# Spectra kept in DRAM twice, once for each half of the partitions, in the hyena stage of a Fourier and Hyena layer

## The chip, the cores and the metric

The kernel runs on one core of a Trainium2 chip. The metric is the device time of one execution in microseconds. Three runs of the kernel before gave 2331.82, 2333.49 and 2336.78; the median, 2333.49, is the time before.

## The reference

One layer works on x of 2048 positions and 1024 channels, in float32. After an RMS norm and an input projection, 512 channels go through a two-dimensional Fourier transform and 512 through a Hyena mixer: two rounds of a gated long convolution, each with a filter that is as long as the sequence. Both results are normed and projected out, added to x, and a feed-forward part with a squared ReLU and a last norm follow. What the change touches is the long convolution:

```
def implicit_filters(l, w0, b0, w_inner, b_inner, freq, w_out):
    z, t = positional_features(l)
    ...
    h = jnp.sin(fr * (z @ w0.astype(f32) + b0.astype(f32)))
```

The filters come out of a small network of the position and a decay over time, in two directions, are normed by their sum of squares, and are convolved with the gated input by way of their spectra: transform of the input, product with the filter's spectrum, inverse transform. The kernel computes the spectra once per group of 128 channels and per round, and reads them again when the input is convolved.

## The kernel before

**Two stages.** The function `filters` makes the filters and their spectra in eight units (four groups of 128 channels, `ct`, times two rounds, `n`). The function `hyena` makes the convolutions in eight blocks of the same groups and rounds. Between the two the spectra lie in DRAM, in the scratch tensors `kd` ("spec" in the profile).

**A unit of the filters.** `generate(q)`, q from 0 to 7, makes an eighth of the unit's filter: a load of the decay (`dec`, one for two q, L170 under the helper `load`), four matmuls (`pk`, L504, on TensorE, PE), a product with the decay on VectorE (DVE; `kt`, L508), a split in a high and a low part (a cast to `kh` on ScalarE, ACT, L181; the rest `kl`, L182, on DVE for even q and on GpSimd, POOL, for odd q), a square on ACT (`sqr`, L518; it has one buffer) and its sum on POOL (`acc`, L519). Behind the last q two folds on POOL end the sum (L521, L522). `normalise` then takes that sum through a matmul (`psum_k`, L528) and some small operations on DVE (`vk`, L530, and further). `skip` puts the result into the filter's first element (`pdk`, L544). `stage1(c)`, c from 0 to 7, makes three matmuls each (L189 to L191) and a transpose on DVE (`Gk`, L418). `stage2(q)` makes four matmuls (`pk2`, L572; "pk" in the profile, which leaves digits out), a copy to `ks` on ACT (L575), and for every second q a store to DRAM (L577).

**The order of the filters.** While unit i runs its eight steps of stage one and eight of stage two, the products of unit i + 2 are generated at steps given by a table, `GENERATE`. For units 1 to 5 the norm of unit i + 1 is made at step q = 1 of stage two; for unit 6 at c = 4 of stage one. From unit 5 on the gates are loaded to `zz` (L623) and scaled on POOL and DVE in turns (L557). All loads and stores go out on SyncE (SP), in order. Each engine runs its instructions in the order in which the compiled program has them; that order is drawn up for each kernel by a scheduler, so that it can move where only a transfer is edited.

**A block of the hyena stage.** `first(c)` transforms the input (L666), `second(q)` takes four frequencies at a time: `spectrum(q)` loads `ks` (L652; four buffers), four matmuls make `pz` (L673), ACT makes the turned copy `zs` (L676, L677), and y = pz * ks[0] + zs * ks[1] is made by DVE (L679), POOL (L680) and one of the two (L681). `inverse(q)` (L689) needs y and runs three steps behind `second`. `turn` and `gate` end the block during the next one. In block 7, the last, no first stage of another block lies beside this. Behind it the output projection begins (`pt_y`, L785, out of `yf`, which is loaded and normed on ACT, L802).

**The form of the spectra.** A spectrum as stage two leaves it lies in 128 partitions, 32 x 128 numbers in each; partitions 0 to 63 hold one part of it and partitions 64 to 127 the other (the product treats them as a real and an imaginary part). In the block `ks[:, 0]` holds the one part and `ks[:, 1]` the other, and both are needed in partitions 0 to 63 as well as in 64 to 127. So each half of the partitions is loaded with the same 256 KB, by two transfers.

Of the kernel before, what the change touches and what calls it, by code (L numbers as in the profile page):

```python
# [10 lines left out]
F32 = mybir.dt.float32  # L11
# [116 lines left out]
P = 128  # L128
# [6 lines left out]
def hybrid_block(ctx: ExitStack, tc: tile.TileContext, A, out):  # L135
    nc = tc.nc
# [4 lines left out]
    def scratch(name, shape):  # L141
        return dram.tile(shape, F32, tag=name, name=name)

    gd = [scratch(f"gates{i}", [P, NT, 512]) for i in range(3)]
    kd = [[scratch(f"spec{i}{n}", [P, 32, 128]) for n in range(2)] for i in range(4)]
    wfd = scratch("wfd", [1024, 512])
    embd = scratch("embd", [P, 32, P])
    xtd = [scratch(f"xt{t}", [P, 8, P]) for t in range(NT)]
# [13 lines left out]
    def pool(name, side="left"):  # L162
        return tc.tile_pool(name=name, bufs=1, side=side, reuse_waits="tile")

    def pa(nm):
        return ps.tile([P, 512], F32, tag="a", name=nm, bufs=8)
# [304 lines left out]
    def filters(ctx, fp, gp, zp, zzs, norms, emb, wo, e1k, f2):  # L471
# [9 lines left out]
        p = pa("plongd")  # L481
# [3 lines left out]
        class Unit:  # L485
# [83 lines left out]
            def stage2(self, q):  # L569
                p = pa("pk2")  # L570
                for j in range(4):
                    nc.tensor.matmul(p[:, 128 * j : 128 * j + 128], lhsT=f2[:, 4 * q + j, :], rhs=self.G[:, :, 4 * q + j], start=True, stop=True)  # L572
                if q % 2 == 0:
                    self.ks = sp.tile([P, 8, 128], F32, tag="ks", name="ks", bufs=3)
                nc.scalar.copy(self.ks[:, 4 * (q % 2) : 4 * (q % 2) + 4, :], p.rearrange("p (f c) -> p f c", f=4))  # L575
                if q % 2:
                    nc.sync.dma_start(kd[self.ct][self.n][:, 4 * q - 4 : 4 * q + 4, :], self.ks)  # L577

        units = [Unit(ct, n) for n in range(2) for ct in range(4)]
        for u in units[:2]:  # L580
# [7 lines left out]
        sp = ctx.enter_context(pool("spectra", "right"))  # L588
# [41 lines left out]
    def hyena(hp, wp, rp, zz, e1, b1, f2, a2, out_weights, out_ahead):  # L630
# [6 lines left out]
        class Block:  # L637
# [9 lines left out]
            def spectrum(self, q):  # L647

                ks = hp.tile([P, 2, 4, 128], F32, tag="ks", name="ks", bufs=4)
                src = kd[self.ct][self.n][:, 4 * q : 4 * q + 4, :].rearrange("(s p) f c -> p s f c", s=2)  # L650
                for hf in (slice(0, 64), slice(64, 128)):
                    nc.sync.dma_start(ks[hf], src)  # L652
                if q == 0:

                    nc.scalar.copy(ks[64:65, 0, 0, :], ks[64:65, 1, 0, :])
                    for h in (0, 64):
                        nc.gpsimd.memset(ks[h : h + 1, 1, 0, :], 0.0)
                return ks
# [742 lines left out]
```

## Time and profile before

| what | before |
|---|---|
| median of three runs | 2333.49 us |
| the profiled execution | 2339.88 us |
| its span | 2336.8 us |
| mean granted TensorE clock | 0.986 |
| stores of spectra | 32 of 512 KB, first issued at 484.7 us, last at 637.5 us |
| loads of spectra | 128 of 256 KB, first issued at 638.0 us, last at 840.2 us |
| HBM read, written | 312.54 MB, 152.27 MB |

The span is the stretch of the profile in which the core works; all times of views count from its start. A group in the profile is a line of the kernel, an engine, an operation and its tiles (out<-in), then how often, busy time and the mean of one in ns, and the idle time of the engine just before such instructions with what ended it. In the view of waits a row tells which engine waited at which line, for whom, how long in total, how often, and the longest. In the timeline a row has its start, its duration, and in brackets how long the engine had been idle and what released it.

### The profile page before, as it was taken

To read this page: it belongs to the slowest core of one execution; us is meant where nothing else is said; L and a number is where in the kernel's file an instruction comes from. 1 tells how busy PE (TensorE), PEld (TensorE's weight loads), DVE (VectorE), ACT (ScalarE), POOL (GpSimd) and SP (SyncE) were. 2 spreads that over 40 slices of the span, in tenths; PEclk is the share of its full clock that TensorE was granted. 3 is DMA by queue.
4 is the path that set the end of the run, shared out by engine and by line. 5 is a ranking of instruction groups with operands and counts; after the bars stand their busy time and mean duration, and the time that the engine had idled before them with its cause. 6 is when DMAs were issued, how large, how long until landed. Compare 5 with 4: busy or idle time off the path is not lost. (4 is left out here: it accounts for less than half of the span.)

```text
span 2336.8 us, 31028 instructions
## 1 busy us (share of the span) xinstructions
PE 2250.9 (96%) x11025; PEld 1860.4 (80%) x11025; DVE 1514.5 (65%) x2248; ACT 1106.6 (47%) x1826; POOL 840.6 (36%) x633
## 2 busy tenths in 40 slices
PE   7999998999899979998999999999999999999998
PEld 6887787799787858886788877888888888888886
DVE  6998666677577774547544457444466666866667
ACT  6554211466455554544555556555543333533334
POOL 3345322567465522215755556555400000000000
PEclk9999999999999989999999999999999999999999
DMA  7535888457688986567544456444479666866631
GB/s 250 181 137 176 290 308 321 144 199 233 214 201 188 200 218 189 177 182 237 161 150 152 152 204 208 152 150 149 149 279 373 234 191 198 284 207 193 198 117 72
DMA packets 294780, 468.42 MB, mean 200 GB/s; under 512 B 18453, under 2 KB 142687, under 8 KB 290273
## 3 DMA queue, kind: packets, MB, share of 16 engines
q1 hardware_dynamic: 291265, 460.43, 61.9%
q10 hardware_dynamic: 3360, 6.02, 0.8%
q8 instruction: 86, 1.41, 0.3%
q14 instruction: 69, 0.57, 0.1%
HBM read 312.54 MB, written 152.27 MB: 199 GB/s over the span
## 5 line engine op out<-in xcount | busy, mean ns | idle before, releaser
L181 ACT CAST qahm<-ra 128x1024 fp32r<-128x1024 f32 x110 | 116.0, 1054 | 345.8 <-PE p2u L190 172.0
L182 DVE TENSOR_TENSOR qalm<-ra,qahm 128x1024 fp32r<-128x1024 f32 x110 | 134.7, 1224 | 154.8 <-ACT qahm L181 151.7
L1183 POOL TENSOR_TENSOR acc<-acc,gfin 128x512 f32<-128x512 f32 x4 | 5.1, 1278 | 632.9 <-DMA out<-acc 625.4
L189 PE MATMUL pu<-wh,xh 128*128 128x512 f32 x512 | 206.4, 404 | 5.8 <-ACT wh L184 4.8
L190 PE MATMUL pu<-wl,xh 128*128 128x512 f32 x512 | 203.3, 397 | 5.9 <-DVE wl L182 3.7
L191 PE MATMUL pu<-wh,xl 128*128 128x512 f32 x512 | 203.2, 397 | 5.7 <-DVE xl L182 5.7
L190 PE MATMUL p2u<-qblm,qahm 128*128 128x512 f32 x504 | 196.2, 389 | 0.3 <-DVE qblm L182 0.3
L189 PE MATMUL p2u<-qbhm,qahm 128*128 128x512 f32 x504 | 195.9, 389 | 0.0
L191 PE MATMUL p2u<-qbhm,qalm 128*128 128x512 f32 x504 | 195.8, 389 | 0.0
L397 POOL TENSOR_TENSOR acc<-acc,cw 128x512 f32<-128x512 f32 x45 | 60.9, 1353 | 206.1 <-DVE acc L374 204.8
L182 DVE TENSOR_TENSOR qblm<-rb,qbhm 128x1024 fp32r<-128x1024 f32 x110 | 134.0, 1219 | 1.1 <-ACT qbhm L181 1.1
L181 ACT CAST ahm<-s 128x512 fp32r<-128x512 f32 x124 | 76.7, 621 | 94.0 <-PE p1v L190 54.1
L190 PEld LDWEIGHTS pu<-wl,xh 128*128 128x128 f32 x512 | 98.3, 192 | 28.7 <-DVE wl L182 4.1
L191 PEld LDWEIGHTS pu<-wh,xl 128*128 128x128 f32 x512 | 98.2, 192 | 28.3 <-DVE xl L182 7.7
L189 PEld LDWEIGHTS pu<-wh,xh 128*128 128x128 f32 x512 | 98.0, 192 | 27.8 <-ACT wh L184 6.2
L182 POOL TENSOR_TENSOR alm<-W,ahm 128x512 fp32r<-128x512 f32 x63 | 85.5, 1358 | 91.4 <-ACT ahm L181 91.4
L181 ACT CAST qbhm<-rb 128x1024 fp32r<-128x1024 f32 x110 | 115.3, 1048 | 4.6 <-DMA a1m<-c 2.8
L190 PEld LDWEIGHTS p2u<-qblm,qahm 128*128 128x128 f32 x504 | 94.6, 188 | 20.3 <-DVE qblm L182 0.8
L189 PEld LDWEIGHTS p2u<-qbhm,qahm 128*128 128x128 f32 x504 | 94.6, 188 | 20.2 <-issue 0.3
L191 PEld LDWEIGHTS p2u<-qbhm,qalm 128*128 128x128 f32 x504 | 94.6, 188 | 19.6
L181 ACT CAST ahm<-W 128x512 fp32r<-128x512 f32 x94 | 57.6, 615 | 103.4 <-PE p1u L190 100.8
L191 PE MATMUL p1u<-bm,alm 128*128 128x512 f32 x252 | 99.9, 396 | 6.4 <-DVE alm L182 6.4
(387 smaller groups left out, 6456.8 us busy)
## 6 DMA issues: line engine op xcount, KB each, us to landing
W<-in_w_fc SPq DMA_DIRECT2D x66, 512.0 KB, 4.6
ks<-spec SPq DMA_DIRECT2D x128, 256.0 KB, 6.8
rb<-td SPq DMA_DIRECT2D x64, 512.0 KB, 4.1
ra<-a1m SPq DMA_DIRECT2D x56, 512.0 KB, 6.0
ra<-a0m SPq DMA_DIRECT2D x54, 512.0 KB, 10.7
rb<-in_w_fc SPq DMA_DIRECT2D x46, 512.0 KB, 4.5
f<-in_w_fc SPq DMA_DIRECT2D x16, 1024.0 KB
td<-f SPq DMA_DIRECT2D x16, 1024.0 KB, 4.7
```

The source lines that it names most:

```text
L181: nc.scalar.copy(hi, src)
L182: (eng or nc.vector).tensor_sub(lo, src, hi)
L189: nc.tensor.matmul(o, lhsT=lh, rhs=rh, start=start, stop=False, skip_group_check=more)
L190: nc.tensor.matmul(o, lhsT=lh, rhs=rl, start=False, stop=False, skip_group_check=more)
L191: nc.tensor.matmul(o, lhsT=ll, rhs=rh, start=False, stop=stop, skip_group_check=more)
L397: nc.gpsimd.tensor_add(m1, m1, cw[:, 3, :])
L1183: nc.gpsimd.tensor_mul(acc[i][:, c], acc[i][:, c], gfin[:, c])
```

## The change

The scratch tensor of a spectrum gets another form, [2, 64, 8, 2, 512], and holds everything twice: the first index h is the half of the partitions that will read it, then come 64 partitions, eight q, the half s of the spectrum, and 512 numbers (four frequencies of 128 channels). In `stage2` each q has a `ks` tile of its own, half as wide as before and with six buffers in place of three. Its two halves of 64 partitions are stored by one transfer each, which reads its source twice (a broadcast over h) and writes 64 x 2 runs of 2 KB. In `spectrum` one transfer takes the place of two: for each of the 128 partitions one run of 4 KB that holds both halves of four frequencies.

So 32 stores of 512 KB become 128 stores of 256 KB, and 128 loads of 256 KB become 64 of 512 KB. SP issues 32 transfers more in all. Lines behind the new empty line have a number higher by one in the changed kernel up to the loads.

```diff
-    kd = [[scratch(f"spec{i}{n}", [P, 32, 128]) for n in range(2)] for i in range(4)]
+
+    kd = [[scratch(f"spec{i}{n}", [2, 64, 8, 2, 512]) for n in range(2)] for i in range(4)]
...
-                if q % 2 == 0:
-                    self.ks = sp.tile([P, 8, 128], F32, tag="ks", name="ks", bufs=3)
-                nc.scalar.copy(self.ks[:, 4 * (q % 2) : 4 * (q % 2) + 4, :], p.rearrange("p (f c) -> p f c", f=4))
-                if q % 2:
-                    nc.sync.dma_start(kd[self.ct][self.n][:, 4 * q - 4 : 4 * q + 4, :], self.ks)
+                ks = sp.tile([P, 1, 512], F32, tag="ks", name="ks", bufs=6)
+                nc.scalar.copy(ks[:, 0], p)
+                for s in range(2):
+                    part = ks[64 * s : 64 * s + 64].broadcast_to([64, 2, 512])
+                    nc.sync.dma_start(kd[self.ct][self.n].rearrange("h p q s x -> p h q s x")[:, :, q, s], part)
...
-                src = kd[self.ct][self.n][:, 4 * q : 4 * q + 4, :].rearrange("(s p) f c -> p s f c", s=2)
-                for hf in (slice(0, 64), slice(64, 128)):
-                    nc.sync.dma_start(ks[hf], src)
+                src = kd[self.ct][self.n].rearrange("h p q s x -> (h p) q (s x)")[:, q]
+                nc.sync.dma_start(ks.rearrange("p s f c -> p (s f c)"), src)
```

The order on PE is the same in both kernels. On DVE, ACT, POOL and SP it changes from unit 1 of the filters to the end of the hyena stage. Three places are shown.

First DVE, around the start of stage one of unit 4 in the kernel before. Gk_4981 is the tile of unit 4's transposes, kt_4946 and kt_4972 are the last two products (q = 6 and 7) of unit 5, and kt_5012 to kt_5070 the first four of unit 6.

```order
L508 TENSOR_TENSOR kt_4946<-pk_4941,dec_4939 128x512
L182 TENSOR_TENSOR kl_4771<-kt_4946,kh_4770 128x4x8x16
L508 TENSOR_TENSOR kt_4972<-pk_4967,dec_4939 128x512
L418 STREAM_TRANSPOSE Gk_4981<-pk1_4982 128x8x2x32
...
L508 TENSOR_TENSOR kt_5012<-pk_5007,dec_5005 128x512
L418 STREAM_TRANSPOSE Gk_4981<-pk1_5019 128x8x2x32
L182 TENSOR_TENSOR kl_5003<-kt_5012,kh_5002 128x4x8x16
...
L508 TENSOR_TENSOR kt_5034<-pk_5029,dec_5005 128x512
L508 TENSOR_TENSOR kt_5058<-pk_5053,dec_5051 128x512
L508 TENSOR_TENSOR kt_5070<-pk_5065,dec_5051 128x512
```

The same place in the changed kernel. Gk_5045 is unit 4's tile there; kt_4936 to kt_5036 are the products q = 4 to 7 of unit 5, and vk_5161 is made of psum_k, the norm of unit 5.

```order
L419 STREAM_TRANSPOSE Gk_5045<-pk1_5046 128x8x2x32
L419 STREAM_TRANSPOSE Gk_5045<-pk1_5051 128x8x2x32
L509 TENSOR_TENSOR kt_4936<-pk_4931,dec_4929 128x512
L509 TENSOR_TENSOR kt_4966<-pk_4961,dec_4929 128x512
L419 STREAM_TRANSPOSE Gk_5045<-pk1_5056 128x8x2x32
L183 TENSOR_TENSOR kl_4819<-kt_4936,kh_4818 128x4x8x16
...
L419 STREAM_TRANSPOSE Gk_5045<-pk1_5110 128x8x2x32
L509 TENSOR_TENSOR kt_5006<-pk_5001,dec_4999 128x512
L509 TENSOR_TENSOR kt_5036<-pk_5031,dec_4999 128x512
L183 TENSOR_TENSOR kl_4819<-kt_5006,kh_4818 128x4x8x16
L531 TENSOR_SCALAR vk_5161<-psum_k_5159 128x1
```

The products q = 4 and 5 of unit 5 moved from ahead of unit 4's first transpose to behind its second, and q = 6 and 7 to behind its last, directly ahead of the norm that needs their squares. Units 2, 3 and 5 have q = 6 and 7 at the same place.

Second ACT, at the same stretch of the program, before: casts and squares of the same products (kh_4770, sqr_4950 and sqr_4976), of the first ones of unit 6 (kh_5002), and the first two copies of unit 4's stage two (ks_5082, twice).

```order
L181 CAST kh_4770<-kt_4946 128x4x8x16
L518 ACTIVATE sqr_4950<-kt_4946 128x512
L575 COPY ks_4958<-pk2_4953 128x512
L575 COPY ks_4958<-pk2_4960 128x512
L181 CAST kh_4770<-kt_4972 128x4x8x16
L518 ACTIVATE sqr_4976<-kt_4972 128x512
...
L575 COPY ks_5082<-pk2_5077 128x512
L518 ACTIVATE sqr_5074<-kt_5070 128x512
L575 COPY ks_5082<-pk2_5084 128x512
```

In the changed kernel, where kh_4818 is unit 5's tile, and ks_5146 and ks_5155 are the first two copies of unit 4's stage two:

```order
L182 CAST kh_4818<-kt_4936 128x4x8x16
L519 ACTIVATE sqr_4940<-kt_4936 128x512
L182 CAST kh_4818<-kt_4966 128x4x8x16
L519 ACTIVATE sqr_4970<-kt_4966 128x512
L575 COPY ks_5146<-pk2_5141 128x512
L575 COPY ks_5155<-pk2_5150 128x512
L182 CAST kh_4818<-kt_5006 128x4x8x16
L519 ACTIVATE sqr_5010<-kt_5006 128x512
L182 CAST kh_4818<-kt_5036 128x4x8x16
L519 ACTIVATE sqr_5040<-kt_5036 128x512
```

The last two casts and squares of unit 5 moved from ahead of unit 4's stage one to behind its first two copies of stage two.

Third POOL, at the norm that unit 6 makes at c = 4 of its stage one, for unit 7. Before, acc_5256 is unit 7's sum of squares and zz_5402 the gates; the last sum and the two folds end it.

```order
L519 TENSOR_TENSOR acc_5256<-acc_5256,sqr_5378 128x512
L557 TENSOR_TENSOR zz_5402<-zz_5402,norms_3591 128x4x128 x2
L519 TENSOR_TENSOR acc_5256<-acc_5256,sqr_5399 128x512
L182 TENSOR_TENSOR kl_5255<-kt_5424,kh_5254 128x4x8x16
L519 TENSOR_TENSOR acc_5256<-acc_5256,sqr_5428 128x512
L521 TENSOR_TENSOR acc_5256<-acc_5256 128x256
L522 TENSOR_TENSOR acc_5256<-acc_5256 128x128
L557 TENSOR_TENSOR zz_5402<-zz_5402,norms_3591 128x4x128 x2
```

In the changed kernel the sum is acc_5336, sqr_5445 to sqr_5520 are the squares of its last four products, and zz_5492 the gates.

```order
L520 TENSOR_TENSOR acc_5336<-acc_5336,sqr_5445 128x512
L183 TENSOR_TENSOR kl_5335<-kt_5462,kh_5334 128x4x8x16
L520 TENSOR_TENSOR acc_5336<-acc_5336,sqr_5466 128x512
L520 TENSOR_TENSOR acc_5336<-acc_5336,sqr_5489 128x512
L183 TENSOR_TENSOR kl_5335<-kt_5516,kh_5334 128x4x8x16
L520 TENSOR_TENSOR acc_5336<-acc_5336,sqr_5520 128x512
L558 TENSOR_TENSOR zz_5492<-zz_5492,norms_3591 128x4x128
L522 TENSOR_TENSOR acc_5336<-acc_5336 128x256
L558 TENSOR_TENSOR zz_5492<-zz_5492,norms_3591 128x4x128
L523 TENSOR_TENSOR acc_5336<-acc_5336 128x128
L558 TENSOR_TENSOR zz_5492<-zz_5492,norms_3591 128x4x128 x6
```

The two scalings of zz that stood together ahead of the last two sums stand between the folds now. On DVE the products of which these squares are made stood ahead of unit 6's first transpose before, and stand behind its fifth now. On SP, the load of the inverse transform's matrix (a2) stood ahead of the stores of units 6 and 7 and stands behind all stores now, directly ahead of the loads of spectra; the reads of yf (L776, L778) moved from behind the last load to the second block.

## The prediction

> **What bounds the kernel now.** The page's first part comes first: TensorE (PE) is busy for nearly the whole span, so time can only be won or lost where PE waits.
>
> ```profile
> span 2336.8 us, 31028 instructions
> PE 2250.9 (96%) x11025; PEld 1860.4 (80%) x11025; DVE 1514.5 (65%) x2248; ACT 1106.6 (47%) x1826; POOL 840.6 (36%) x633
> ```
>
> The change touches two stages, which the windows view separates: the filters (stores, about 484 to 637 us) and the hyena blocks (loads, 638 to 860 us). Its columns: stretch, then busy time of PE, PEld, DVE, ACT, POOL, the granted clock, the share of the DMA engines, GB/s.
>
> ```profile
> 500.00:560.00 60.00, 60.00 (x459) 55.33 (x458) 42.83 (x81) 38.77 (x79) 44.91 (x38) 1.00 0.63 210
> 600.00:620.00 20.00, 12.99 (x69) 10.14 (x69) 11.77 (x23) 6.62 (x14) 10.04 (x9) 0.83 0.48 176
> 640.00:840.00 200.00, 188.22 (x1314) 163.55 (x1312) 150.41 (x234) 110.67 (x192) 116.55 (x104) 0.99 0.88 198
> 840.00:860.00 20.00, 13.68 (x64) 9.39 (x64) 10.58 (x21) 6.95 (x16) 5.08 (x4) 0.74 0.98 261
> ```
>
> In the filters PE has no gap at all from 500 to 560 us; every wait added there is added to the end. In the hyena blocks PE lacks 11.8 us up to 840 and 6.3 us in the last 20, with the DMA engines at 0.88 and 0.98. The waits view of 640 to 870 us says on what (engine and line waited, releaser: us in total, times, longest):
>
> ```profile
> PE pv L689 <- DVE y L681: 16.0, 15, 3.8
> PE pt_y L785 <- ACT yf L802: 4.1, 2, 3.1
> POOL zs L680 <- DMA ks<-spec: 30.6, 18, 6.0
> DVE y L679 <- DMA ks<-spec: 12.1, 13, 3.5
> PE pv L689 <- DVE y L681: 7.3, 7, 1.6
> ```
>
> The last line is the same view for 830 to 855 us alone. PE waits for y, and y's two inputs wait for the spectra, so the loads are what is late.
>
> **The loads (gain).** Today a load of four frequencies is two DMAs, each to 64 partitions. In the list of DMA issues (KB each, us to landing) they stand beside two transfers between DRAM and 128 partitions in runs of 4 KB, which is the new load's form:
>
> ```profile
> ks<-spec SPq DMA_DIRECT2D x128, 256.0 KB, 6.8
> spec<-ks SPq DMA_DIRECT2D x32, 512.0 KB, 3.7
> dec<-in_decay SPq DMA_DIRECT2D x32, 512.0 KB, 4.0
> ```
>
> The new load should land in about 4.0 us, as dec does, while it moves both halves. Per byte it should also hold the engines for less. In 500 to 560 us, where all traffic is of 128 partitions, a share of 0.63 moves 210 GB/s, 333 GB/s at full share. In 640 to 840 us, mostly 64-partition loads, 0.88 moves 198, 225 at full share. So 512 KB hold the engines for 2.3 us now and 1.6 us then. With that, y should come in time. The 8.7 us that PE waits for y before 830 go (16.0 less 7.3). Of the 7.3 us in the last block, which has no first stage to cover its chain of y, I take half, 3.6. The changed order issues the reads of yf and their norm in the second block instead of behind the last load, so the 4.1 us at pt_y go too. With 0.6 us for matmuls at a lower clock after such waits I take -17. Bounds: -4 (only pt_y), and -24 (16.0 + 4.1 and all 4 us or so of slow clock, which the 0.74 in the last slice suggests).
>
> **The stores: the order they make (loss).** The arithmetic of each step stays. The copy to ks is 128x512 as before, and the second copy of the spectra is made by the DMA. But 128 small stores in place of 32 lie ahead of the loads of dec on SP, and the order of DVE, ACT and POOL is drawn up anew round them. In units 2 to 5 the last products kt (q6 and q7) of the unit after now stand behind all eight transposes of this unit on DVE, and their casts and squares behind the first two ks copies on ACT (the rows of order in the section on the change). Before, they stood ahead of the transposes. Yet PE's order is as it was: after the second group of stage two comes psum_k, which needs the sum of all squares. PE's timeline of unit 1 gives the clock of a unit (start, us, ...):
>
> ```profile
> 491.94 0.48 PE L189 MATMUL pk<-k,e1h 128*128 128x512 f32 x1
> ...
> 499.41 1.95 PE L504 MATMUL pk<-wo,emb 128*128 128x128 f32 x16
> ...
> 502.98 0.28 PE L528 MATMUL psum_k<-ones,acc 128*128 128x1 f32 x2
> ```
>
> Count from a unit's first matmul: stage one is through at 7.5 us, and psum_k, behind two groups of stage two, is asked for at 11.0. Durations for the chain come from the groups of 484 to 640 us (busy, mean ns):
>
> ```profile
> L519 POOL TENSOR_TENSOR acc<-acc,sqr 128x512 f32<-128x512 f32 x40 | 52.3, 1307 | 12.5 <-ACT sqr L518 12.5
> L418 DVE STREAM_TRANSPOSE Gk<-pk 128x512 f32<-128x512 f32 x56 | 37.9, 702 | 4.7 <-PE pk L191 4.7
> L575 ACT COPY ks<-pk 128x512 f32<-128x512 f32 x63 | 35.0, 579 | 11.7 <-PE pk L572 11.6
> L508 DVE TENSOR_TENSOR kt<-pk,dec 128x512 f32<-128x512 f32 x44 | 29.6, 675 | 9.1 <-PE pk L504 6.8 <-ACT ks L575 1.2 <-POOL kl L182 0.8
> L518 ACT ACTIVATE sqr<-kt 128x512 f32<-128x512 f32 x40 | 25.3, 632 | 15.7 <-POOL acc L519 15.7
> L182 POOL TENSOR_TENSOR kl<-kt,kh 128x512 fp32r<-128x512 f32 x19 | 24.9, 1311 | 11.2 <-ACT kh L181 11.2
> L181 ACT CAST kh<-kt 128x512 fp32r<-128x512 f32 x36 | 22.3, 618 | 25.8 <-DVE kt L508 25.8
> L557 POOL TENSOR_TENSOR zz<-zz,norms 128x512 f32<-128x512 f32 x8 | 12.5, 1581 | 10.4 <-ACT norms L553 9.8 <-PE pk L572 0.6
> L521 POOL TENSOR_TENSOR acc<-acc 128x256 f32<-128x256 f32 x6 | 4.4, 737 | 0.5
> L522 POOL TENSOR_TENSOR acc<-acc 128x128 f32<-128x128 f32 x6 | 3.3, 548 | 0.5
> ```
>
> The eighth transpose ends at 8.4 us, kt of q6 and q7 at 9.1 and 9.8. That is early enough, but ACT must first copy ks of q0 and q1, the second of them at 11.0 to 11.6. Then cast to 12.2, square to 12.9; POOL adds to 14.2, splits q7 (1.31) to 15.5, adds its square to 16.8, and folds in 0.74 and 0.55 to 18.1. PE waits from 11.0 to 18.1. Successive operations overlap a little, so I take 7.0. Nothing of PE's is left to fill it: the next matmuls stand behind psum_k. DVE too has its next products behind the result (vk). So it comes again in each of units 2 to 5.
>
> The trace has one such wait already, in unit 6, with what follows it on PE:
>
> ```profile
> 599.27 0.48 PE L189 MATMUL pk<-kh,e1h 128*128 128x512 f32 x1
> ...
> 602.39 0.40 PE L190 MATMUL pk<-kl,e1h 128*128 128x512 f32 x1
> 609.21 0.59 PE L528 MATMUL psum_k<-ones,acc 128*128 128x1 f32 x2 [6.20 <-POOL acc L522]
> ...
> 610.65 0.63 PE L191 MATMUL pk<-kh,e1l 128*128 128x512 f32 x1
> ...
> 613.21 0.58 PE L191 MATMUL pk<-kh,e1l 128*128 128x512 f32 x1
> ```
>
> The 14 matmuls of stage one before it follow each other by 0.24 us (3.12 us for 13 steps, between the first two rows), those behind it by 0.43 (2.56 us for 6 steps, between the last two; the slice's clock is 0.83). For the nine matmuls of the three groups that end at 613 that is 9 x 0.19 = 1.7 us, lost behind a wait of this length. Units 2 to 5: 4 x (7.0 + 1.7) = **+35**. Bounds 20 (5 us each, no slow clock) and 40.
>
> In unit 6 psum_k is asked for 3.7 us after the unit's start and ran at 9.9 (609.21 less 599.27). Before, all eight kt stood ahead of this unit's transposes on DVE; now five transposes stand ahead of the last four kt. The fifth ends at 4.4, kt of q4 at 5.1, cast and square at 6.3. From there POOL is the chain, as its order shows: four sums and two splits (6 x 1.31; the third sum starts 0.7 late, behind a square that waits for its one buffer) to 14.8, then zz, fold, zz, fold (1.58 + 0.74 + 1.58 + 0.55) to 19.2. **+9**; bounds 5 and 12.
>
> **The stores as transfers.** They double from 16.8 to 33.6 MB, read 64 partitions at a time. The DMA view of 484 to 640 us and of 640 to 840 us, and SP's issues:
>
> ```profile
> q1 hardware_dynamic: 16095, 33.78, 64.0%
> q1 hardware_dynamic: 32014, 39.34, 87.2%
> L577 SPq DMA_DIRECT2D spec<-ks x32: 319/320/1562, 484.7 to 637.5; - x32
> L652 SPq DMA_DIRECT2D ks<-spec x128: 573/605/4610, 638.0 to 840.2; - x128
> ```
>
> At 333 GB/s the stage's 33.8 + 16.8 MB need 152 us of engine time. If reads from 64 partitions go like today's writes to 64 (225 GB/s), it is 33.6/225 + 17.0/333 = 200 us. The stage lasts 153 us now and with the waits above some 197, so either nearly fits. SP issues 128 x 0.6 = 77 us in that time. What stays is the end: unit 7 makes its 16 stores (4.2 MB) in about 7 us, and a2 (2.1 MB) comes behind all of them, where it stood ahead of them before. That is 6.3 MB, 19 to 25 us at the two rates, ahead of the first load of spectra: 12 to 18 us more than the 7 us in which they are made, 8 to 14 more than the 4 us that it takes to land. The first y was multiplied at 647.3 while the load was issued at 638.0:
>
> ```profile
> 647.28 0.65 DVE L679 TENSOR_TENSOR y<-pz,ks 128x512 f32<-128x512 f32 x1
> ```
>
> With a landing of 4 to 5 us some 4 us of the 9.3 between are spare. I take **+5**, bounds 0 and 14. The nearer row is that of the 512 KB stores (3.7 us), which read SBUF too.
>
> The Trainium skill, "DMA: Bandwidth & Descriptors", Rules for kernel authors, says that two transfers to disjoint partition halves serialize on the same 16 engines and that one 128-partition transfer should be used. It speaks for the new load and against the new store, and gives halves no lower rate of their own: by it the stores cost 152 us of engine time and the sum is the one below, while by the trace's 225 GB/s it would be 9 us more.
>
> **The sum.** +35 + 9 + 5 - 17 = +32 on the profiled execution of 2339.9 us (span 2336.8 and 3.1 around it): 2371.9. That execution lies 6.4 us above the median of 2333.5, so on the median's scale 2365.5.
>
> **The rivals.** *Half-rate stores* (0.19): the stores go at 225 GB/s, and PE finds DMA 3 us behind (200 against 197) and the first load some 10 later than it can bear: +35 + 9 + 14 - 17 = +41, 2374.5. For it: 0.88 share at 198 GB/s; against: those were writes to SBUF. *The load gains nothing* (0.12): the engines' time goes by bytes, the bytes are the same, and only pt_y is won: +35 + 9 + 5 - 4 = +45, 2378.5. Then the change wouldn't do what it says. Against it: 4.0 against 6.8 us. *Faster* (0.13): the chain of squares runs ahead of what I worked out, so that PE does not wait at psum_k in units 2 to 5, the first load is not late, and the loads give their full -24: -24 + 9 = -15, 2318.5. It decides from where the wait per unit is below (24 - 9 - 5)/4 = 2.5 us. For it: DVE has 29% of its time free in 500 to 560 us. Against: the ks copies alone end at 11.6, after psum_k is asked for, and a cast, a square, two sums and two folds must follow (1.25 + 2.6 + 1.3 = 5.2 us).
>
> **How the numbers follow.** My forecast has 0.56. Its lower end is 20 + 5 + 0 - 23 = +2 (2335.5) and its upper 40 + 12 + 14 - 12 = +54 (2387.5). The faster case stays mostly outside below, and about 0.07 above. A change under 0.2% (4.7 us) cannot be told from none here: faster 0.13; same 0.06, from the forecast's lower end; slower 0.81.
>
> **What would show it.** In the changed trace: a wait of psum_k for POOL's acc of about 7 us in units 2 to 5 and some 15 in unit 6; units of 28 to 30 us instead of 21; ks loads landing in about 4 us, DMA share in the blocks down from 0.88 to about 0.6; the wait for y below 5 us; no wait at pt_y. I am wrong if psum_k waits under 3 us per unit, if stores land so late that ACT waits for a ks buffer, or if PE's wait for y stays.

## The result and the profile after

The changed kernel takes 2385.38 us (median of four runs, 2382.82 to 2389.84) against 2335.14 us of the kernel before on the same chips: a ratio of 1.0221, 95% interval 1.0203 to 1.0240. It is 50 us slower. The forecast was 32 us slower (2365.5, with a range up to 2387.5): the sign was right, and so were the waits that were named in the filters and in the blocks; the size was 18 us short.

The page of the changed kernel and its list of issues:

```profile
span 2383.4 us, 31063 instructions
PE 2261.7 (95%) x11025; PEld 1871.1 (79%) x11025; DVE 1509.3 (63%) x2248; ACT 1109.6 (47%) x1826; POOL 841.8 (35%) x633
...
spec<-ks SPq DMA_DIRECT2D x128, 256.0 KB, 4.2
ks<-spec SPq DMA_DIRECT2D x64, 512.0 KB, 3.8
```

The work of PE is the same (its busy time grew by 11 us, at a lower clock); the loads land in 3.8 us in place of 6.8 and bring twice as much. The windows of the filters, of the end of that stage, and of the blocks (busy time of PE, PEld, DVE, ACT, POOL, clock, DMA share, GB/s):

```profile
500.00:560.00 60.00, 46.21 (x323) 41.30 (x322) 29.91 (x56) 28.38 (x54) 28.62 (x24) 0.94 0.75 234
640.00:706.00 66.00, 39.66 (x214) 33.41 (x213) 28.64 (x43) 15.41 (x29) 22.07 (x16) 0.77 0.70 207
720.00:880.00 160.00, 160.00 (x1138) 140.98 (x1137) 129.37 (x211) 99.58 (x174) 107.67 (x96) 0.99 0.74 227
```

The filters lost what they had: PE, without a gap before, is busy for 46 of 60 us. The blocks won: from 720 to 880 PE has no gap. The waits view of PE names both (484 to 660 us, then 715 to 915 us):

```profile
PE psum_k L529 <- POOL acc L523: 42.4, 5, 15.1
PE pz L673 <- DVE y L679: 4.9, 1, 4.9
PE pb L702 <- ACT yh L182: 3.8, 1, 3.8
PE pv L689 <- DVE y L681: 0.8, 1, 0.8
```

PE's wait for y at pv was 16.0 us and is 0.8, and psum_k costs 42.4 in five waits. The 4.9 us stand at the very first y (716 us) and belong to the late start of the blocks. The wait of 4.1 us at pt_y for yf is gone, but 3.8 us for yh stand right behind that place now (to 911.9 us), where PE had no wait before. The chain behind one of the waits at psum_k, in unit 5, which begins at 606.12, from the timelines of ACT, POOL and PE:

```profile
616.95 0.58 ACT L575 COPY ks<-pk 128x512 f32<-128x512 f32 x1 [1.20 <-PE pk L573]
617.44 0.62 ACT L182 CAST kh<-kt 128x512 fp32r<-128x512 f32 x1
617.96 0.63 ACT L519 ACTIVATE sqr<-kt 128x512 f32<-128x512 f32 x1
```

```profile
618.66 1.26 POOL L520 TENSOR_TENSOR acc<-acc,sqr 128x512 f32<-128x512 f32 x1 [4.13 <-ACT sqr L519]
619.89 1.27 POOL L183 TENSOR_TENSOR kl<-kt,kh 128x512 fp32r<-128x512 f32 x1
621.11 1.27 POOL L520 TENSOR_TENSOR acc<-acc,sqr 128x512 f32<-128x512 f32 x1
622.45 0.72 POOL L522 TENSOR_TENSOR acc<-acc 128x256 f32<-128x256 f32 x1
623.25 0.45 POOL L523 TENSOR_TENSOR acc<-acc 128x128 f32<-128x128 f32 x1
```

```profile
615.86 1.06 PE L573 MATMUL pk<-Gk,f 128*128 128x128 f32 x8
623.76 0.58 PE L529 MATMUL psum_k<-ones,acc 128*128 128x1 f32 x2 [6.84 <-POOL acc L523]
624.21 2.05 PE L505 MATMUL pk<-wo,emb 128*128 128x128 f32 x8
626.05 1.91 PE L573 MATMUL pk<-Gk,f 128*128 128x128 f32 x8
```

POOL had been idle for 4.1 us when the first square came; that square stood on ACT behind the second ks copy, which is where the order had put it. The two groups behind the wait take 2.05 and 1.91 us in place of 1.06; the granted clock of 623.7 to 628.5 us is 0.56.

Where the 46.6 us of the two spans (2383.4 and 2336.8) lie, by the starts of PE's and DVE's rows in the two timelines:

| stretch | before | after | difference |
|---|---|---|---|
| start to unit 2 | 512.9 | 511.2 | -1.6 |
| units 2 to 5 | 86.4 | 125.6 | +39.2 |
| units 6 and 7 | 37.4 | 49.2 | +11.7 |
| end of unit 7 to the first y | 10.6 | 30.3 | +19.7 |
| first y to the first pt_y | 214.7 | 190.7 | -24.0 |
| the rest | 1474.8 | 1476.4 | +1.6 |

While PE waits for the first y it works ahead on other matmuls, so a border at the first y makes the rows on both sides of it a little too large. With the border at the first pv of PE (652.58 us before, 719.25 after; PE's order is the same), the end of the stage loses 17.4 us and the blocks win 21.6.

### The profile page after: what moved, and what is told of

Read it like the earlier page. It is cut to its first block, busy times and chain, and to the rows that moved or that the text cites. A ratio compares the mean times of both kernels' runs of the same rounds, so it can differ in the third digit from the quotient of the medians.

```text
span 2383.4 us, 31063 instructions
## 1 busy us (share of the span) xinstructions
PE 2261.7 (95%) x11025; PEld 1871.1 (79%) x11025; DVE 1509.3 (63%) x2248; ACT 1109.6 (47%) x1826; POOL 841.8 (35%) x633
## 4 chain that ended last, share of the span: by engine, by line
PE 77%; DMA 7%; DVE 6%; ACT 3%; issue 3%; POOL 3%; SPq 1%; ACTq 0%; DVEq 0%; POOLq 0%
PE p1u L192 5%; PE p1u L190 5%; PE p1u L191 5%; PE p2u L191 5%; PE p2u L190 5%; PE p2u L192 5%; PE pu L192 3%; PE pu L191 3%; PE pu L190 3%; PE p2v L190 2%; PE p2v L191 2%; PE p2v L192 2%; DMA f<-in_w_fc 2%; PE p1v L190 2%; PE p1v L191 2%
## 5 line engine op out<-in xcount | busy, mean ns | idle before, releaser
L190 PEld LDWEIGHTS pu<-wh,xh 128*128 128x128 f32 x512 | 98.2, 192 | 29.3 <-ACT wh L185 5.7
L192 PEld LDWEIGHTS p2u<-qbhm,qalm 128*128 128x128 f32 x504 | 94.6, 188 | 19.7
L190 PE MATMUL p1u<-bm,ahm 128*128 128x512 f32 x252 | 100.2, 398 | 5.9 <-ACT ku L1046 5.9
```

Of the source, the lines that this page charges most:

```text
L190: nc.tensor.matmul(o, lhsT=lh, rhs=rh, start=start, stop=False, skip_group_check=more)
L192: nc.tensor.matmul(o, lhsT=ll, rhs=rh, start=False, stop=stop, skip_group_check=more)
```

## The experiments

**Loads by halves again, from the doubled spectra (e3).** Only the load differs from the changed kernel:

```diff
-                nc.sync.dma_start(ks.rearrange("p s f c -> p (s f c)"), src)
+                for h in range(2):
+                    nc.sync.dma_start(ks[64 * h : 64 * h + 64].rearrange("p s f c -> p (s f c)"), kd[self.ct][self.n][h, :, q].rearrange("p s x -> p (s x)"))
```

> The changed kernel with its loads taken apart again: two of 64 partitions per four frequencies, from the doubled spectra, in runs of 4 KB; stores and their order as in the changed kernel. Theory (a transfer to 64 partitions holds the DMA engines longer per byte, and the hyena blocks gained 20 us from the one load): the gain goes, landing 6 us or more, 2400 to 2408. Rival (run length, not the number of partitions, sets the price): the loads land in 4 to 5 us and the time stays at 2385 to 2390.

Measured: 2409.3 us, ratio to before 1.0312 (1.0288 to 1.0336). The issue line, and the window of 720 to 900 us:

```profile
ks<-spec SPq DMA_DIRECT2D x128, 256.0 KB, 7.1
```

```profile
720.00:900.00 180.00, 171.09 (x1171) 147.34 (x1172) 131.71 (x205) 98.66 (x171) 109.90 (x98) 0.97 0.83 197
```

The run is of 4 KB, the number of partitions 64: landing is 7.1 us again, and 0.83 of the engines move 197 GB/s, 237 at full share, where the changed kernel's 0.74 move 227, 307 at full share. From the first y to pt_y it takes 212.2 us in place of 190.7. So the price of the old load is not its run, and the one load is worth some 21 us, all of the gain: from the first pv to pt_y it takes 209.3 us, 209.4 before and 187.8 in the changed kernel. What differs between this run and the changed kernel is the 64 partitions, and with them a transfer of half the size; no run parts these two, though stores of the same 256 KB moved 295 GB/s at full share (e5, below), which speaks for the partitions.

**The old stores, the load cut by parts in place of halves (e4).**

```diff
-                for hf in (slice(0, 64), slice(64, 128)):
-                    nc.sync.dma_start(ks[hf], src)
+                for s in range(2):
+                    src = kd[self.ct][self.n][64 * s : 64 * s + 64, 4 * q : 4 * q + 4, :].rearrange("p f c -> p (f c)")
+                    nc.sync.dma_start(ks[:, s].rearrange("p f c -> p (f c)"), src.unsqueeze(0).broadcast_to([2, 64, 512]))
```

> The kernel before with its stores and the form of the spectra untouched; only the two loads of four frequencies are cut the other way: each brings one part to all 128 partitions, reading its source twice, in place of both parts to 64 partitions. Same number, same bytes, runs of 2 KB. Theory (64 partitions are the price): landing below 5 us, PE's wait for y below 8 us, 10 to 20 us faster than before: 2315 to 2325. Rival (the larger transfer and the longer run make the gain): 2333 to 2337, landing 6 to 7 us. A third case: a source read twice by one transfer goes over few engines, then far slower, above 2400.

Measured: 2842.5 us. The third case. SP's issues and the DMA view of 720 to 900 us:

```profile
L652 SPq DMA_DIRECT2D ks<-spec x128: 479/5082/11329, 639.2 to 1336.3; - x128
```

```profile
DMA packets 6906, 10.22 MB, mean 57 GB/s; under 512 B 145, under 2 KB 2705, under 8 KB 6902
q1 hardware_dynamic: 6902, 10.17, 16.4%
```

One issue takes 5.1 us on SP, and the engines are busy for 0.16 of the time at 57 GB/s: most of them stand still. The Trainium skill, "DMA: Bandwidth & Descriptors", Rules for kernel authors, has this: an outermost step of fewer than 16, such as a source repeated by a leading zero step, confines the whole transfer to at most as many engines. The two copies are such a step of 2, and the run agrees. So this run says nothing on partitions, and it shows why a second copy in DRAM was a way to the one load at all.

**dec ahead of the stores on SP (e1).** A test of my reason: the waits at psum_k come from the order, so the old order should bring the time back.

```diff
+                    with tc.high_priority(offset=400):
-                    self.dec = load(fp, "dec", [P, 8, 128], A["decay"][self.ct][:, 4 * q : 4 * q + 8, :], 2)
+                        self.dec = load(fp, "dec", [P, 8, 128], A["decay"][self.ct][:, 4 * q : 4 * q + 8, :], 2)
```

> The changed kernel with the loads of dec given a higher priority and nothing else. On DVE the products kt then stand ahead of the transposes again, as in the kernel before, in all units; stores and loads of spectra keep their new form. My theory (the order costs the time in the filters): PE waits at psum_k in unit 6 alone, about 6 us, units 2 to 5 take 21 to 22 us each in place of 31, so some 45 to 50 us come back; but the doubled stores now have to go in 153 us in place of 200, so the first load of spectra may be up to 20 us later still: 2335 to 2358. Rival (the doubled transfers cost the time, the order only shows it): units 2 to 5 stay above 25 us because ACT waits for ks buffers or DVE for dec, 2370 or more.

Measured: 2390.7 us, ratio 1.0232 (1.0205 to 1.0259), no better than the changed kernel. The kt stand where they stood before and no wait at psum_k is left, yet units 2 to 5 take 128 us. Two rows of the waits of 484 to 700 us, SP's own and ACT's, and SP's timeline at the end of unit 3 (unit 4 begins at 577.0):

```profile
SPq L171 <- DVE kt L510: 75.9, 20, 7.1
ACT ks L576 <- DMA spec<-ks: 32.8, 17, 5.7
```

```profile
569.06 0.96 SPq L579 DMA_DIRECT2D spec<-ks  x1
577.01 0.33 SPq L171 DMA_DIRECT2D dec<-in_decay  x1
577.40 3.22 SPq L579 DMA_DIRECT2D spec<-ks  x4
```

SP stands from 570 to 577 us at a load of dec that waits until DVE's kt frees its buffer, with stores behind it, and in all 75.9 us in 20 such waits. Where stores are held up, ACT lacks ks buffers, and its copies hold up the casts and squares behind them. (Of ACT's 32.8 us only 7.5 lie in units 2 to 5; the rest comes behind them, where e5 waits as well.) The theory as I had put it fell: the order is one of two ways in which stores and dec hold each other up on one queue, and each costs about the same.

**zz and a2 ahead as well (e2).** The same priority for the loads of zz and a2:

```diff
-                        nc.sync.dma_start(zzs[0][:, :, cs], gd[0][:, :, cs])
+                        with tc.high_priority(offset=400):
+                            nc.sync.dma_start(zzs[0][:, :, cs], gd[0][:, :, cs])
...
-    a2 = load(tp, "a2", [P, 32, P], A["a2"])
+    with tc.high_priority(offset=400):
+        a2 = load(tp, "a2", [P, 32, P], A["a2"])
```

> As the run with dec first, and the loads of zz and a2 have the higher priority too, so that they stand ahead of the stores of units 6 and 7 on SP. Theory (of the 20 us that lie between the end of unit 7 and the first y beyond those of before, most is the place of zz and a2 behind the stores): the first y comes 12 to 18 us behind unit 7's end, 10.6 before; 10 to 20 us faster than with dec alone, 2318 to 2345. Rival (the bytes of the stores are the backlog, wherever zz and a2 stand): within 5 us of the run with dec first.

Measured: 2388.15 us (ratio 1.0221, 1.0196 to 1.0247). Within 5 us of e1; ACT waits 35.2 us for ks buffers. The first y comes 25.9 us behind unit 7's end, 35.6 in e1: a gain of 9.7, but 12 to 18 us were expected, and units 2 to 5 took 3.5 us more. With SP held up as above it can't tell more.

**dec on another queue (e5).** The changed kernel with dec issued from ACT:

```diff
-                    self.dec = load(fp, "dec", [P, 8, 128], A["decay"][self.ct][:, 4 * q : 4 * q + 8, :], 2)
+                    self.dec = fp.tile([P, 8, 128], F32, tag="dec", name="dec", bufs=2)
+                    nc.scalar.dma_start(self.dec, A["decay"][self.ct][:, 4 * q : 4 * q + 8, :])
```

> The changed kernel with the loads of dec issued from ACT in place of SP, nothing else: dec no longer stands behind stores, nor stores behind dec. The order of kt on DVE is again that of the kernel before. With dec first on SP the waits at psum_k went but ACT waited 33 us for ks buffers while SP stood at loads of dec, so two theories are left. One queue (stores and dec hold each other up on SP, in either order): units 2 to 5 take 21 to 24 us each, ACT waits under 10 us for ks buffers, 2335 to 2355, the rest being the end of the stage. Stores themselves (16 stores per unit with six buffers of half the size can't keep up with 21 us): ACT goes on waiting for ks, units above 28 us, 2375 or more.

Measured: 2348.28 us, ratio 1.0064 (1.0043 to 1.0084), some 37 us less than the changed kernel with all its stores and bytes. Units 2 to 5 take 95.4 us (unit 5 alone 29.3), units 6 and 7 35.3. In units 2 to 5 DVE's kt stand as in e1; what differs is dec's queue. Windows of the filters, of their end and of the blocks, and of 500 to 560 us the DMA queues (q1 is SP's with the stores, q10 ACT's with dec: packets, MB, share):

```profile
500.00:560.00 60.00, 58.66 (x445) 53.74 (x445) 40.80 (x79) 37.04 (x73) 43.37 (x36) 1.00 0.86 274
620.00:680.00 60.00, 40.75 (x220) 32.70 (x218) 19.89 (x25) 12.26 (x23) 12.37 (x8) 0.86 0.95 292
700.00:860.00 160.00, 159.59 (x1146) 138.36 (x1146) 132.96 (x218) 100.86 (x176) 103.76 (x91) 1.00 0.72 220
```

```profile
q1 hardware_dynamic: 5749, 10.46, 59.0%
q10 hardware_dynamic: 1629, 5.90, 27.0%
```

That settles one queue against the stores themselves for units 2 to 5, in which ACT never waits for a ks buffer. It settles the half rate too: 274 GB/s at 0.86 are 319 at full share, near the 333 of before, and the stores alone moved 295 (10.46 MB in 0.59 of 60 us), so a store that reads 64 partitions is not much slower per byte, unlike a load that writes 64. What is left is the end: 37.0 us from unit 7's end to the first y (10.6 before), with the DMA engines at 0.95, and ACT waits 22.4 us for ks buffers from 640 to 690. PE now runs ahead of the transfers.

**zz and a2 on ACT too (e6).**

```diff
-                        nc.sync.dma_start(zzs[0][:, :, cs], gd[0][:, :, cs])
+                        nc.scalar.dma_start(zzs[0][:, :, cs], gd[0][:, :, cs])
...
-    a2 = load(tp, "a2", [P, 32, P], A["a2"])
+    a2 = tp.tile([P, 32, P], F32, tag="a2", name="a2")
+    nc.scalar.dma_start(a2, A["a2"])
```

> As the run with dec on ACT, and zz and a2 are issued from ACT as well, so that on SP only stores stand ahead of the loads of spectra. One queue: the 20 us between unit 7's end and the first y beyond those of before shrink to 5 to 10, so 8 to 15 us faster than with dec alone on ACT. Stores themselves: their backlog alone delays the first load, within 4 us of the run with dec on ACT.

Measured: 2348.32 us (1.0062, 1.0039 to 1.0084), equal to e5. First y 28.7 us behind unit 7's end, but units 2 to 5 took 105.8. The 8 to 15 us that were expected did not come. The bytes are the same; what was won at one place was lost at another, and why units 2 to 5 took longer was not tested.

**Half as many stores (e7).** ks holds two q, and the spectra are laid out for pairs of q:

```diff
-    kd = [[scratch(f"spec{i}{n}", [2, 64, 8, 2, 512]) for n in range(2)] for i in range(4)]
+    kd = [[scratch(f"spec{i}{n}", [2, 64, 4, 2, 1024]) for n in range(2)] for i in range(4)]
...
+                for s in range(2 if q % 2 else 0):
+                    part = self.ks[64 * s : 64 * s + 64].broadcast_to([64, 2, 1024])
+                    nc.sync.dma_start(kd[self.ct][self.n].rearrange("h p r s x -> p h r s x")[:, :, q // 2, s], part)
...
+                src = kd[self.ct][self.n].rearrange("h p r s x -> (h p) r s x")[:, q // 2, :, 512 * (q % 2) : 512 * (q % 2) + 512]
+                nc.sync.dma_start(ks.rearrange("p s f c -> p s (f c)"), src)
```

> As the run with dec on ACT, with half as many stores of twice the size: the spectra are laid out for pairs of q, [2, 64, 4, 2, 1024], ks has three buffers of two q as in the kernel before, a store brings 64 partitions x 2 runs of 4 KB, 512 KB; a load is one transfer to 128 partitions with two runs of 2 KB. If the number of stores costs (issue of 0.75 us each on SP, one wait each): 5 to 15 us faster than with dec on ACT. If only the bytes do: within 4 us of it. Loads should land within 5 us, as the partitions set their price.

Measured: 2359.92 us (1.0110, 1.0088 to 1.0132), 12 us slower than e5 with half the issues, which neither side had expected. Fewer stores win nothing here, and the first y still comes 37.5 us behind unit 7's end; loads with two runs of 2 KB to 128 partitions land in 4.0 us. The larger stores land in 6.9 us, in e5 in 4.7, and hold one of three buffers meanwhile, for which ACT waits 31.9 us from 640 to 690 (22.4 in e5); whether that is all of the 12 us was not tested.

**As many stores, half the bytes (e8).** Only h = 0 is stored, and both halves are loaded from it, as in e3 otherwise:

```diff
-                    part = ks[64 * s : 64 * s + 64].broadcast_to([64, 2, 512])
-                    nc.sync.dma_start(kd[self.ct][self.n].rearrange("h p q s x -> p h q s x")[:, :, q, s], part)
+                    part = ks[64 * s : 64 * s + 64]
+                    nc.sync.dma_start(kd[self.ct][self.n].rearrange("h p q s x -> p h q s x")[:, 0:1, q, s], part)
```

> The spectra stored once (h = 0 alone) by as many stores as in the changed kernel, 128 of 128 KB; loads apart by halves, both from the one copy. To be set beside the run with old loads (2409), which differs in the second copy only. If the bytes of the second copy cost the time: the filters take 155 to 165 us as before, 2335 to 2350. If number and order do: PE waits at psum_k as in the changed kernel, 2390 to 2410.

Measured: 2348.98 us (1.0064, 1.0040 to 1.0088), 60 us below e3. But the shorter stores also moved the order: PE waits at psum_k for 1.3 us in unit 5 and 7.4 in unit 6, not 6.8 in each of four units and 15. So bytes and order fell together, and this run can't part them. It does show that 128 stores beside dec on SP need not cost 39 us by their number: units 2 to 5 took 102.1 us, and the first y came 11.9 us behind unit 7's end.

**The kernel before with dec on ACT (e9).** A control for e5, with the same edit of dec as there.

> The kernel before with dec issued from ACT, stores and loads of spectra untouched: what moving dec is worth by itself. DVE's order of kt is that of the kernel before. If dec's place on SP costs only together with the 128 stores: 2329 to 2338, no change. If it helps by itself, below 2328, and the run with dec on ACT has to be read against it.

Measured: 2341.5 us, ratio 1.0035 (1.0022 to 1.0048). Moving dec to ACT costs 7 us by itself, which neither case had expected; units 2 to 5 take 91.2 us (86.4). Of the 15 us by which e5 lies above before, half may be this, if the two simply add, which was not tested.

**Fewer units kept twice (e10, e11).** As e5, with the spectra of the first six or four units kept twice, and the others stored once and loaded by halves. The stores, for six:

```diff
-                for s in range(2):
+                for s in range(2 if 4 * self.n + self.ct < 6 else 0):
...
+                if 4 * self.n + self.ct >= 6:
+                    nc.sync.dma_start(kd[self.ct][self.n][:, q], ks[:, 0])
```

> As the run with dec on ACT (2348), but only the spectra of units 0 to 5 are kept twice and loaded in one transfer; those of units 6 and 7 are stored once, 256 KB from 128 partitions per q, and loaded by halves in blocks 6 and 7. Theory (with the order repaired, the bytes of the doubled stores at the end of the stage, DMA share 0.94 and more from 620 to 700 us, delay the first y by 26 us): 4.2 MB fewer at the end are 13 us at 316 GB/s, the two blocks give back 5 to 8: 2337 to 2344, with 12 to 16 us between unit 7's end and the first y in place of 37. Rival (the delay comes from SP's queue and latency, not bytes): within 4 us of 2348 or above.

> As the last, with the spectra of units 0 to 3 alone kept twice. Theory: the end of the stage is that of the kernel before (10 to 14 us from unit 7's end to the first y), units 2 to 5 take 21 to 22 us, and half of the gain of 21 to 23 us in the blocks is left, the last block's wait excepted: 2325 to 2333, the first version that is not slower than the kernel before. Rival: the loads by halves in blocks 4 to 7 take the whole gain back: 2334 to 2345.

Measured: 2333.04 us for six (0.9992, 0.9982 to 1.0002) and 2331.79 for four (0.9990, 0.9981 to 0.9999). The first y comes 18.9 and 10.6 us behind unit 7's end, 37.0 in e5. For six units, SP has zz and a2 between and behind the stores as in e5, and half the number of stores with all their bytes gave 37.5 (e7): so it was the bytes at the end of the stage. For four, zz and a2 also go out ahead of unit 7's stores, so the 10.6 are not the bytes' alone. Six came out 4 us below the range that was expected, four inside it. Their loads by halves land in 3.7 and 4.4 us, not in 6.8, and from 740 to 820 us, with such loads alone, the second run's PE has no gap at a DMA share of 0.83: how long a load takes to land does not hang on its form alone. Per byte it holds them as before (194 GB/s, 234 at full share).

**Four units, dec on POOL (e12).** As e11, with dec on a third queue:

```diff
-                    nc.scalar.dma_start(self.dec, A["decay"][self.ct][:, 4 * q : 4 * q + 8, :])
+                    nc.gpsimd.dma_start(self.dec, A["decay"][self.ct][:, 4 * q : 4 * q + 8, :])
```

> As the run with four units kept twice (2331.8), with dec issued from POOL in place of ACT. Moving dec to ACT cost 7 us in the kernel before (2341.5 to 2334.2), since ACT holds dec's issue behind its own waits. If that is the queue's place, POOL, which is busy for 0.74 of its time and ahead of PE in units 2 to 5, may bear it better: 2322 to 2329, clearly faster than the kernel before. If issuing on POOL costs POOL's own time (its sums are what psum_k waits for), waits at psum_k come back: 2335 or more.

Measured: 2322.53 us, ratio 0.9945 (0.9931 to 0.9958): faster than both kernels. PE's waits of 484 to 640 us at psum_k, of 640 to 870 us for y, and a row of POOL's timeline:

```profile
PE psum_k L530 <- POOL acc L524: 0.9, 1, 0.9
PE pv L696 <- DVE y L688: 5.6, 5, 1.9
```

```profile
528.29 0.57 POOL L502 DMA_DIRECT2D dec<-in_decay  x1
```

An issue takes 0.57 us of POOL. From the first y to pt_y it takes 201.1 us (214.7 before), units 6 and 7 30.3 (37.4), units 2 to 5 89.4 (86.4). The time is as expected, its reason is not shown: against e11 units 2 to 5 won nothing (88.8 there), and the 11 us came in units 6 and 7, where e11 waits 10.4 us at psum_k and this run 0.9. Why that wait goes with dec on POOL stays open, and the kernel before with dec on POOL was not run; so of what is won over it, the 7 us in units 6 and 7 may have nothing to do with the spectra.

## Why the prediction was right, and where it was short

**The loads.** Forecast -17 with -24 as a bound; 24.0 us were won from the first y, 21.6 from the first pv. Landing was put at 4.0 and is 3.8 us. The wait for y went further than said (15.2 of 16.0 us, 12.3 were put). Matmuls at a lower clock were put at 0.6 us; from the first pv to pt_y PE is busy for 185.7 us in place of 190.1, so 4.5 came back. The 4.1 us at pt_y were counted as won and were nearly lost again in the 3.8 us for yh behind it. The reason, transfers to 64 partitions, is borne out by e3. The DMA share came to 0.74 and not to 0.6: more was moved in the same time (227 GB/s, 198 before), and full share moved 307 and not the 333 that were taken.

**The order.** Forecast: waits of 7.0 us in each of units 2 to 5 and of some 15 in unit 6. Measured: four of 6.84, and 15.06. The chain of order rows with the durations of before gave the wait to 0.2 us, on ACT, POOL and PE as worked out. Units 2 to 5 lost 39.2 against +35: 27.4 are these waits, and 11.2 are matmuls at a lower clock (PE is busy for 95.9 us in place of 84.6 with the same matmuls, at a clock of 0.89 in place of 1.00), of which some 7 stand in the two groups behind each wait, as forecast. The units took 31 to 33 us, where 28 to 30 were named. Units 6 and 7 lost 11.7 against +9.

**What the order hangs on.** I had taken it as given; e1 shows that another order of the same queue costs as much, and e5 that dec off that queue gives 37 us back. So the cause of these 37 us is that these stores and the loads of dec share SP, each waiting there for another engine; e8 shows that their number alone is not enough. The rival of half-rate stores is out by e5's 295 GB/s, that of a load that gains nothing by e3. The faster one never came near: its point was a wait of 2.5 us per unit.

**The step that failed is the end of the stage, +5 with bounds 0 and 14; it measured +19.7 (17.4 by the first pv).** I worked out 8 to 14 us for the first load and held 4 of them to be spare. One sign of being wrong that I had named came here: stores land so late that ACT waits for a ks buffer. ACT's wait of 640 to 720 us, SP's timeline, the first y of DVE, and the window from unit 7's end to that y:

```profile
ACT ks L575 <- DMA spec<-ks: 9.0, 4, 5.7
```

```profile
676.12 0.66 SPq L624 DMA_DIRECT2D zz<-gates  x1
676.88 10.92 SPq L578 DMA_DIRECT2D spec<-ks  x8
687.84 0.76 SPq L624 DMA_DIRECT2D zz<-gates  x1
688.69 16.02 SPq L578 DMA_DIRECT2D spec<-ks  x14
704.81 1.13 SPq L171 DMA_DIRECT2D a<-in_a  x1
...
706.77 2.51 SPq L652 DMA_DIRECT2D ks<-spec  x4
```

```profile
716.28 0.69 DVE L679 TENSOR_TENSOR y<-pz,ks 128x512 f32<-128x512 f32 x1 [12.86 <-DMA ks<-spec]
```

```profile
686.00:716.00 30.00, 17.23 (x78) 13.90 (x76) 8.39 (x11) 4.21 (x8) 5.80 (x4) 0.83 0.93 309
```

Unit 7 ends at 686.0; the last 14 stores go out behind that, at 1.1 us each, and the first load follows 20.8 us behind the end, not 1.3 as before. I had counted the stores of unit 7 and a2 but not that zz, 4.2 MB, which went out at 563 to 587 us before, now comes in between them, its last part at 687.8. Between the forecast and the two spans lie 14.6 us (18 between the medians): with the border at the first pv the end of the stage was put 12.4 us too low and the order 6.9, and the loads won 4.6 more. That the loads' error took back most of the order's is luck, and so is that the time still came inside the range, 2 us below its upper end. (The range takes -23 and -12 for the loads, where the bounds worked out were -24 and -4; no reason is given.)

The DMA engines are the bound at this place in the changed kernel too: their share of 640 to 706 us is only 0.70, because from 640 to 660, while PE waits at psum_k, it is 0.39; from unit 7's end to the first y it is 0.93. What they move there is stores (4.2 MB), the first loads of spectra (2.1 MB), and zz's last part and a2 (3.1 MB), which had gone out by 599 us before. With zz and a2 ahead the first y came 8 to 10 us sooner at the same bytes (e2 against e1, e6 against e5), with half the bytes in units 6 and 7 it came 18 us sooner (e10 against e5). How the 20 us of the changed kernel itself divide between SP's order and bytes stays open, since each of these runs has other filters.

## What to carry to other kernels

When an edit changes how many transfers a queue issues, read first what else stands on that queue, then the order that the scheduler makes of it: a chain of order rows with durations from the trace gave these waits to a few tenths of a microsecond. To win from transfers to all partitions, count the bytes that their layout adds at the busiest place, with all else that the new order puts there, and keep the second copy only where there is room for it. If a repaired order brings nothing, look on the queue for who waits now, before the theory is given up or kept.

## What the runs showed of the hardware that was not expected

A transfer of 256 KB that repeats its source by an outermost step of 2 went on few engines: 57 GB/s at a share of 0.16, and 5.1 us for its issue on SP (e4). Blocks with loads that write 64 partitions of SBUF moved 225 GB/s (before), 237 (e3, runs of 4 KB) and 234 (e11) at full DMA share, where loads to 128 moved 307; the same loads landed in 6.8 and 7.1 us in the first two and in 4.4 in e11. Stores that read 64 partitions landed in 4.2 us, and moved 295 GB/s at full share on a queue of their own (e5). One in-order queue of transfers whose buffers wait for other engines cost 37 us at the same bytes and the same order of DVE (e1, e5).
